# One hybrid MLA + NSA block on one Trainium2 core: weights' low parts summed by accumulating DMAs, short Newton steps moved to GpSimd, strips loaded a step ahead

## The chip, the cores and the metric

The kernel runs on 1 core of one Trainium2 chip. The metric is device microseconds of one execution. The engines are TensorE (PE; its weight loads are PEld), VectorE (DVE), ScalarE (ACT), GpSimd (POOL) and SyncE (SP), which here only issues DMAs.

## What is computed

A decoder block over 512 tokens with D = 1024, all in float32:

```
mod = silu(c) @ ada_w + ada_b                     # six vectors: shift, scale, gate, twice
h   = rms_norm(x) * (1 + sc1) + sh1
z   = h @ w_in                                    # latents c_q (768), c_kv (256), k_pe, the NSA inputs, two merge gates (2 x 1024)
q   = rms_norm(c_q) @ w_q_b                       # 8 heads x 96;  k, v from rms_norm(c_kv) @ w_kv_b
y_mla = causal_attention(norm_rope(q), norm_rope(k), v) @ w_o_mla
y_nsa = (compressed + selected + window attention) @ w_o_nsa
x   = x + gt1 * ((sigmoid(g1) * y_mla + sigmoid(g2) * y_nsa) @ w_out)
h2  = rms_norm(x) * (1 + sc2) + sh2
out = x + gt2 * ((silu(h2 @ w_gate) * (h2 @ w_up)) @ w_down)
```

## The kernel before

Every matrix product is made of three: both factors are split into a high part, rounded to float32r, and a low part, which is the rest, and high x high, high x low and low x high are summed in PSUM. A weight chunk of up to 128 x 1024 is split by `wchunk`: SP loads `raw`, ACT copies it into `whi` (`hi_of`, which rounds), DVE (or POOL) subtracts to give `wlo` (`lo_of`). `raw`, `whi` and `wlo` have four buffers each (pool `wp`), used in turn by all weights and by the strips of `ada_w` (below), so a load waits until the fourth last user of `raw` is done.

The stages, by the span of the profile: input normalisation and the first modulation vectors; the input projection; NSA attention (some 160 to 302 us); the latent stage, 302 to about 350 us, which projects latents to keys and values (`gk`, `use_kv`) and then queries (`gq`, `use_q`, two halves c = 0 and 1 of four heads each); MLA attention over eight heads (about 350 to 450 us); the merge (`gym`), `w_out` (`gwo`, `wo`), the second normalisation (`make_h2`) and the feed-forward part to the end.

Two kinds of work are laid beside the attention. Fillers are PE work with nothing else to do with it: `gates` (16 chunks of the two merge gates, PSUM tile `gp`) and `y_nsa` (tile `yn`). Their results go through an SBUF tile `gs` to DRAM (`spill`) and come back as `gx`, `gm` and `yn`. Their low parts are made by POOL until the end of NSA, by DVE after it (`fill_on`), in two halves of 128 x 512 (`FILL_CUT`). And `mods` computes the other modulation vectors: it loads strips of `ada_w` and sums them, scaled, into `macc` by DVE. The quotas E_MODS, F_MODS, Y_MODS and W_MODS say how many steps of `mods` go into the latent stage, the MLA heads, the merge and `w_out`.

The root mean square of queries and keys is turned into its inverse by `rsqrt`: a guess from the bits and three Newton iterations on a 128 x 16 tile (`rq_i`, `rq_h`, `rq_m`). `rsk` scales the keys `kn`; `rsq` is the scale in the DVE instruction that reads a score tile `ps` out of PSUM and gives `s` and its minimum `mn`.

The program order is not the order of the code: the framework schedules the instructions when it builds, engine by engine, from estimated durations, and each engine then runs its own list strictly in that order. An instruction that waits holds up all behind it on its engine, a DMA issue too.

## Time and profile before

| | |
|---|---|
| median of 3 runs (range) | 886.44 us (884.62 to 892.15) |
| the profiled execution | 885.92 us, of which the span from first to last instruction is 884.1 us |
| PE busy | 842.3 us, 95% of the span |
| DVE / ACT / POOL busy | 681.2 / 451.9 / 98.3 us |
| mean granted TensorE clock | 0.987 of full speed |

All times in the rows below are microseconds from the first instruction of the profiled execution, unless marked ns. An engine's busy time counts what it computes, not the DMAs that it issues.

### The profile page before, as it was taken

What the parts mean: (1) busy time and instruction counts of PE and PEld (TensorE: products, weight loads), DVE (VectorE), ACT (ScalarE), POOL (GpSimd) and SP (SyncE); (2) the same over time, 40 slices, a digit from 0 to 9 for tenths busy, and PEclk for the clock granted to TensorE, in tenths of its full rate; (3) what the DMA queues carried; (4) which work ended last, traced back from release to release, by engine and by line L of the source; (5) the groups of instructions that cost most, each with busy time, mean ns of one, the idle gap of its engine ahead of it and who ended that gap; (6) DMA issues with size and microseconds to landing.
All of it is one profiled execution on the core that took longest, in us unless ns stands there. A gap on an engine that the chain in (4) does not pass through costs nothing.

```text
span 884.1 us, 13839 instructions
## 1 busy us (share of the span) xinstructions
PE 842.3 (95%) x5012; PEld 740.3 (84%) x5012; DVE 681.2 (77%) x1438; ACT 451.9 (51%) x902; POOL 98.3 (11%) x146
## 2 busy tenths in 40 slices
PE   5999899899999999799899989999999999999997
PEld 4889899678777788688788879898999889988996
DVE  5858786678987599679779885996788768865875
ACT  5445664686766564466534255452366326641550
POOL 0004235343442000001010000000000000000000
PEclk9999999799999999899999999999999999999999
DMA  9934455312100455225589762534233413343312
GB/s 314 320 111 125 138 149 137 84 48 61 49 25 24 151 172 172 90 88 164 169 275 314 232 212 73 160 126 121 69 98 97 143 48 97 108 131 96 96 49 95
DMA packets 96217, 115.53 MB, mean 131 GB/s; under 512 B 6564, under 2 KB 68884, under 8 KB 96148
## 3 DMA queue, kind: packets, MB, share of 16 engines
q1 hardware_dynamic: 96052, 114.62, 41.9%
q8 instruction: 39, 0.64, 0.3%
q14 instruction: 30, 0.25, 0.1%
q10 hardware_dynamic: 96, 0.03, 0.0%
...
## 4 chain that ended last, share of the span: by engine, by line
PE 76%; DVE 10%; DMA 8%; ACT 2%; issue 2%; POOL 1%; SPq 1%; DVEq 0%; ACTq 0%
PE d L143 14%; PE fx L143 12%; PE fy L143 9%; PE gp L143 9%; PE ga L143 5%; PE pt L143 3%; PE av L143 3%; DMA raw<-in_ada_w_dram 3%; PE gwo L143 3%; PE gym L143 3%; PE fg L143 3%; PE fu L143 3%; PE wo L143 2%; DVE wlo L143 2%; PE wa L143 2%
## 5 line engine op out<-in xcount | busy, mean ns | idle before, releaser
L143 ACT ACTIVATE whi<-raw 128x1024 fp32r<-128x1024 f32 (+4 forms) x162 | 142.0, 893 | 146.5 <-PE d L143 49.3
L143 DVE TENSOR_TENSOR wlo<-raw,whi 128x1024 fp32r<-128x1024 f32 (+4 forms) x138 | 149.4, 1089 | 65.8 <-ACT whi L143 65.6
L143 PE MATMUL d<-wlo,mh 128*128 128x512 f32 (+1 forms) x180 | 70.7, 393 | 0.0
L143 PE MATMUL d<-whi,mh 128*128 128x512 f32 (+1 forms) x180 | 69.5, 392 | 0.6 <-DVE tm L143 0.5
L143 PE MATMUL d<-whi,ml 128*128 128x512 f32 (+1 forms) x180 | 67.8, 389 | 0.0
L143 ACT ACTIVATE s<-s,mn 128x384 f32<-128x384 f32 (+2 forms) x96 | 52.5, 548 | 26.0 <-DVE mn L143 23.5
L143 DVE TENSOR_TENSOR plo<-pt,phi 128x512 fp32r<-128x512 f32 (+2 forms) x78 | 46.3, 601 | 20.4 <-ACT phi L143 20.1
L143 ACT ACTIVATE phi<-pt 128x512 fp32r<-128x512 f32 (+2 forms) x78 | 40.1, 526 | 33.3 <-PE pt L143 32.7
L143 PE MATMUL gp<-hTh,whi 128*128 128x512 f32 x128 | 55.2, 431 | 0.0
L143 PE MATMUL gp<-hTh,wlo 128*128 128x512 f32 x128 | 51.5, 404 | 0.0
L143 PE MATMUL gp<-hTl,whi 128*128 128x512 f32 x128 | 51.4, 401 | 0.0
L143 ACT ACTIVATE whi<-s 128x1024 fp32r<-128x1024 f32 (+1 forms) x36 | 30.2, 845 | 32.3 <-PE d L143 18.0
L143 POOL TENSOR_SCALAR s<-s,sm 128x512 f32<-128x512 f32 (+3 forms) x40 | 25.0, 637 | 152.7 <-DVE sm L143 67.8
L143 PE MATMUL fx<-h2h,whi 128*128 128x256 f32 x144 | 41.2, 286 | 0.0
L143 PEld LDWEIGHTS d<-whi,mh 128*128 128x128 f32 x180 | 33.7, 188 | 8.9 <-DVE tm L143 1.2
L143 PE MATMUL fx<-h2h,wlo 128*128 128x256 f32 x144 | 40.9, 284 | 0.0
L143 PE MATMUL fx<-h2l,whi 128*128 128x256 f32 x144 | 40.8, 283 | 0.0
L143 PEld LDWEIGHTS d<-whi,ml 128*128 128x128 f32 x180 | 33.8, 188 | 7.9 <-issue 0.2
L143 PEld LDWEIGHTS d<-wlo,mh 128*128 128x128 f32 x180 | 33.8, 188 | 7.7 <-issue 0.2
L143 DVE TENSOR_TENSOR wlo<-s,whi 128x1024 fp32r<-128x1024 f32 (+1 forms) x36 | 33.8, 950 | 7.4 <-ACT whi L143 7.4
L143 DVE SCALAR_TENSOR_TENSOR macc<-raw,csil,macc 128x512 f32<-128x512 f32 x45 | 33.6, 753 | 5.6 <-DMA raw<-in_ada_w_dram 5.3
L143 PE MATMUL pt<-ident,s 128*128 128x128 f32 x232 | 37.8, 282 | 0.0
...
## 6 DMA issues: line engine op xcount, KB each, us to landing
...
araw<-in_ada_w_dram SPq DMA_DIRECT2D x32, 256.0 KB, 6.3
...
spill<-gs SPq DMA_DIRECT2D x24, 256.0 KB, 2.0
...
```

The lines of the kernel that those rows point to most:

```text
L143: out = call(*args, **kw)
```

## The change

- `sum_lo` is new: ACT writes the negated, rounded weights into `wlo`, and a DMA that POOL issues adds `raw` to them in place. It replaces DVE's subtraction in the query projection (`eng_lo=sp` is the mark for it) and, after NSA, in the fillers.
- `rsqrt` can run its Newton steps on another engine: POOL for the keys (`k0`, `k1`) and the queries (`q0`, `q1`). There it takes 12 steps where DVE took 9.
- `use_q` copies all 96 columns of a head out of PSUM by ACT; DVE's rotation then reads SBUF.
- Spills are issued by ACT (gates) and POOL (`yn`), no longer by SP.
- `mods` gives way between a strip's load and its sums, with all quotas doubled to match.
- The low parts of the second half of the first gate and up weights wait until the second piece of `h2` is done.

```diff
@@ -38,11 +38,11 @@
 E0_GATES = 8
 E_GATES = 0
 F_FILL = 64
-E_MODS = 4
-F_MODS = 4
+E_MODS = 8
+F_MODS = 8
 GS_BUFS = 1
-Y_MODS = 4
-W_MODS = 4
+Y_MODS = 8
+W_MODS = 8
 BIG = 1e30
 QL = 768
 KVL = 256
@@ -206,7 +206,8 @@
     pe.transpose(pt[:, :56], vec, ident[:56, :56])
     dve.tensor_copy(out=cols, in_=pt[:, :56])
 
-    def rsqrt(dst, src, pool_, tag):
+    def rsqrt(dst, src, pool_, tag, eng=None):
+        eng = eng or dve
         n = src.shape[-1]
         rows = src.shape[0]
         yi = pool_.tile([P, n], I32, name=f"rq_i_{tag}", tag=f"rq_i{n}", bufs=2)[:rows]
@@ -216,10 +217,14 @@
         dve.tensor_scalar(out=hx, in0=src, scalar1=-0.5, scalar2=None, op0=ALU.mult)
         y = yi.bitcast(F32)
         for it in range(3):
-            dve.tensor_tensor(out=m, in0=y, in1=hx, op=ALU.mult)
-            dve.tensor_tensor(out=m, in0=m, in1=y, op=ALU.mult)
+            eng.tensor_tensor(out=m, in0=y, in1=hx, op=ALU.mult)
+            eng.tensor_tensor(out=m, in0=m, in1=y, op=ALU.mult)
             o = dst if it == 2 else y
-            dve.scalar_tensor_tensor(out=o, in0=m, scalar=1.5, in1=y, op0=ALU.add, op1=ALU.mult)
+            if eng is dve:
+                dve.scalar_tensor_tensor(out=o, in0=m, scalar=1.5, in1=y, op0=ALU.add, op1=ALU.mult)
+            else:
+                eng.tensor_scalar(out=m, in0=m, scalar1=1.5, scalar2=None, op0=ALU.add)
+                eng.tensor_tensor(out=o, in0=m, in1=y, op=ALU.mult)
 
     ss = cst.tile([P, NT + 1], F32, name="ss")
     rstd = cst.tile([P, NT], F32, name="rstd")
@@ -249,6 +254,10 @@
                 act.activation(out=v, in_=v, func=AF.Copy, scale=rstd[:, t : t + 1])
 
     scale_x(0, P)
+
+    def sum_lo(dst, src):
+        act.activation(out=dst, in_=src, func=AF.Copy, scale=-1.0)
+        pool.dma_start(out=dst, in_=src, accum_op=ALU.add)
 
     def wchunk(src, parts, n, eng_lo=None, cut=1):
         raw = wp.tile([P, 1024], F32, name="raw", tag="raw")
@@ -260,7 +269,10 @@
         for i in range(cut):
             c = slice(i * m, (i + 1) * m)
             hi_of(h[:, c], raw[:, c])
-            lo_of(l[:, c], raw[:, c], h[:, c], eng_lo)
+            if eng_lo is sp:
+                sum_lo(l[:, c], raw[:, c])
+            else:
+                lo_of(l[:, c], raw[:, c], h[:, c], eng_lo)
         return (h[:, : parts * n].rearrange("p (a n) -> p a n", a=parts),
                 l[:, : parts * n].rearrange("p (a n) -> p a n", a=parts))
 
@@ -867,9 +879,10 @@
             gs = wp.tile([P, 1024], F32, name="gs", tag="raw")[:, :S]
         if gate is None:
             act.activation(out=gs, in_=ps, func=AF.Tanh, scale=0.5)
+            act.dma_start(out=spilled[at // 4][at % 4], in_=gs)
         else:
             dve.scalar_tensor_tensor(out=gs, in0=gate, scalar=1.0, in1=ps, op0=ALU.add, op1=ALU.mult)
-        sp.dma_start(out=spilled[at // 4][at % 4], in_=gs)
+            pool.dma_start(out=spilled[at // 4][at % 4], in_=gs)
 
     def ahead(jobs, lead=1, eng=lambda: ()):
         ready = [wchunk(*job, *eng()) for job in jobs[:lead]]
@@ -946,6 +959,7 @@
                 for r0 in range(0, KD, 2):
                     raw = strip()
                     sp.dma_start(out=raw.rearrange("p (r n) -> p r n", r=2), in_=rows(ada, r0 * P, 2, m * D + hf * S, S))
+                    yield
                     for r in range(2):
                         src = raw[:, r * S : (r + 1) * S]
                         c = csil[:, r0 + r : r0 + r + 1]
@@ -1072,7 +1086,7 @@
     nsa_last = pe.log[-1]
     spill_src.clear()
     pe.pace = 0
-    fill_on[0] = dve
+    fill_on[0] = sp
     tab_st.close()
 
     mc_st = scope()
@@ -1126,13 +1140,13 @@
                 pv = ps.rearrange("p (h d) -> p h d", h=4)
                 jq = mp.tile([P, 4, MQK], F32, name="jq", tag="jq", bufs=2)
                 act.activation(out=jq, in_=pv, func=AF.Square)
-                act.activation(out=qn[t][:, hs, 0:64], in_=pv[:, :, 0:64], func=AF.Copy)
+                act.activation(out=qn[t][:, hs, :], in_=pv, func=AF.Copy)
                 rot = mp.tile([P, 4, 32], F32, name="rot", tag="rot", bufs=2)
                 heads = lambda v: v.unsqueeze(1).broadcast_to([P, 4, v.shape[-1]])
                 qr = qn[t][:, hs, 64:96]
-                dve.tensor_tensor(out=rot[:, :, 0:16], in0=pv[:, :, 80:96], in1=heads(snq[:, t, 0:16]), op=ALU.mult)
-                dve.tensor_tensor(out=rot[:, :, 16:32], in0=pv[:, :, 64:80], in1=heads(snq[:, t, 16:32]), op=ALU.mult)
-                dve.tensor_tensor(out=qr, in0=pv[:, :, 64:96], in1=heads(c2q[:, t, :]), op=ALU.mult)
+                dve.tensor_tensor(out=rot[:, :, 0:16], in0=qr[:, :, 16:32], in1=heads(snq[:, t, 0:16]), op=ALU.mult)
+                dve.tensor_tensor(out=rot[:, :, 16:32], in0=qr[:, :, 0:16], in1=heads(snq[:, t, 16:32]), op=ALU.mult)
+                dve.tensor_tensor(out=qr, in0=qr, in1=heads(c2q[:, t, :]), op=ALU.mult)
                 dve.tensor_tensor(out=qr, in0=qr, in1=rot, op=ALU.add)
                 dve.tensor_reduce(out=msq[:, c, t, :], in_=jq, axis=AX.X, op=ALU.add)
             return f
@@ -1140,7 +1154,7 @@
         def norm_q(c):
             hs = slice(4 * c, 4 * c + 4)
             dve.scalar_tensor_tensor(out=msq[:, c], in0=msq[:, c], scalar=1.0 / MQK, in1=each_t(vq, 4), op0=ALU.mult, op1=ALU.add)
-            rsqrt(flat(rsq[:, c]), flat(msq[:, c]), mt, f"q{c}")
+            rsqrt(flat(rsq[:, c]), flat(msq[:, c]), mt, f"q{c}", pool)
             yield
 
         def use_kv(c):
@@ -1159,7 +1173,7 @@
                     mk, rk = msk[:, c], rsk[:, c]
                     dve.tensor_tensor(out=mk, in0=mk, in1=each_t(rkv2, 4), op=ALU.mult)
                     dve.tensor_tensor(out=mk, in0=mk, in1=each_t(skp, 4), op=ALU.add)
-                    rsqrt(flat(rk), flat(mk), mp, f"k{c}")
+                    rsqrt(flat(rk), flat(mk), mp, f"k{c}", pool)
                     for u in range(NT):
                         dve.tensor_tensor(out=kn[u][:, hs, 64:96], in0=kpr[:, u : u + 1, :].broadcast_to([P, 4, 32]),
                                           in1=rsk[:, c, u, :].unsqueeze(2).broadcast_to([P, 4, 32]), op=ALU.mult)
@@ -1176,7 +1190,7 @@
         qk_st = scope()
         qkp = qk_st.enter_context(tc.tile_pool(name="qkp", bufs=2, reuse_waits="tile"))
         for c in range(2):
-            with_side(gemm_tok(sel_ct(0), a["mla_w_q_b"][0], 6, 384 * c, 384, use_q(c), tag=f"q{c}"))
+            with_side(gemm_tok(sel_ct(0), a["mla_w_q_b"][0], 6, 384 * c, 384, use_q(c), tag=f"q{c}", eng_lo=sp))
             if c == 0:
                 run(norm_q(0))
 
@@ -1411,8 +1425,10 @@
                     act.activation(out=h2, in_=src, func=AF.Identity, scale=a2, bias=b2)
                     hi_of(hi, h2)
                 lo_of(lo, h2, hi)
-            yield
-
+            h2_done.append(dve.last)
+            yield
+
+    h2_done = []
     act.gate = act.last
     act.activation(out=warm, in_=ones[:, 0:1], func=AF.Silu)
     act.gate = None
@@ -1599,7 +1615,9 @@
             for k0 in range(0, KD, 4):
                 for nm, w in GU:
                     if q == 0:
+                        dve.gate = h2_done[1] if k0 > 0 else None
                         wt[nm, k0] = wchunk(rows(w, k0 * P, 4, 0, 256), 4, 256)
+                        dve.gate = None
                     gu_matmuls(ps, nm, k0, wt[nm, k0], slice(2 * q * P, (2 * q + 2) * P), q == 0)
                     yield ps
 
@@ -1670,7 +1688,7 @@
                         next(slabs)
                         gated_sums()
                     finish_mid(0, sg_first)
-                run(mix((slabs, 6), (part(mods_gen, 4), 4)))
+                run(mix((slabs, 6), (part(mods_gen, 8), 8)))
         if i == 0:
             run(mods_gen)
             need_mod(5)
```

How it moves instructions. Names: `macc` and `raw<-in_ada_w` belong to `mods`, `ql` and `kl` are low parts of a head's queries and keys, `jq` holds squares, `ISA s,mn<-ps` reads a score tile.

DVE where the first MLA scores are read, before:

```order
L143 TENSOR_SCALAR rq_i_q_4266<-msq 128x16
L143 TENSOR_SCALAR rq_h_q_4267<-msq 128x16
L143 TENSOR_TENSOR rq_m_q_3926<-rq_m_q_3926,rq_i_q_3924 128x16
L143 SCALAR_TENSOR_TENSOR kl<-pt,cols_688,kh 96x512
L143 SCALAR_TENSOR_TENSOR macc<-raw,csil,macc 128x512
L143 TENSOR_TENSOR rq_m_q_4268<-rq_i_q_4266,rq_h_q_4267 128x16
L143 SCALAR_TENSOR_TENSOR rsq<-rq_m_q_3926,rq_i_q_3924 128x16
L143 TENSOR_TENSOR wlo<-raw,whi 128x512 x2
L143 SCALAR_TENSOR_TENSOR macc<-raw,csil,macc 128x512
L143 TENSOR_TENSOR rq_m_q_4268<-rq_m_q_4268,rq_i_q_4266 128x16
L143 ISA s_4123,mn<-ps,mask,rsq 128x128
L143 ISA mn 128x1
```

The same place on DVE now:

```order
L143 SCALAR_TENSOR_TENSOR kl<-pt,cols_688,kh 96x512
L143 SCALAR_TENSOR_TENSOR msq<-msq,vq 128x16
L143 TENSOR_TENSOR qn_3486<-qn_3486,c2q 128x4x32
L143 SCALAR_TENSOR_TENSOR macc<-raw,csil,macc 128x512
L143 TENSOR_SCALAR rq_i_q_4290<-msq 128x16
L143 TENSOR_SCALAR rq_h_q_4291<-msq 128x16
L143 TENSOR_TENSOR qn_3486<-qn_3486,rot 128x4x32
L143 SCALAR_TENSOR_TENSOR macc<-raw,csil,macc 128x512
L143 ISA s_4142,mn<-ps,mask,rsq 128x128
L143 ISA mn 128x1
```

The Newton steps and the filler's low parts are gone from DVE ahead of the first score; two strip sums are still ahead of it.

ACT while it empties the first key/value tiles (`gk`) and splits the first query chunks, before:

```order
L143 ACTIVATE jq<-gk_3557 128x4x64
L143 ACTIVATE kn_3488<-gk_3557 128x4x64
L143 ACTIVATE VM_3492<-gk_3557,rkv 128x4x64
L143 ACTIVATE whi<-raw 128x768
L143 ACTIVATE jq<-gk_3558 128x4x64
L143 ACTIVATE kn_3489<-gk_3558 128x4x64
L143 ACTIVATE VM_3493<-gk_3558,rkv 128x4x64
L143 ACTIVATE whi<-raw 128x768
L143 ACTIVATE jq<-gk_3559 128x4x64
```

The same place on ACT now:

```order
L143 ACTIVATE whi<-raw 128x768
L143 ACTIVATE wlo<-raw 128x768
L143 ACTIVATE jq<-gk_3559 128x4x64
L143 ACTIVATE kn_3488<-gk_3559 128x4x64
L143 ACTIVATE VM_3492<-gk_3559,rkv 128x4x64
L143 ACTIVATE jq<-gk_3560 128x4x64
L143 ACTIVATE kn_3489<-gk_3560 128x4x64
L143 ACTIVATE VM_3493<-gk_3560,rkv 128x4x64
L143 ACTIVATE wlo<-raw 128x768
L143 ACTIVATE whi<-raw 128x768
```

Each chunk of the query weights now has two passes of ACT, and they stand between the evictions of the `gk` tiles.

POOL in the same stretch now (none of these rows stood on it before):

```order
L143 TENSOR_TENSOR rq_i_k_3767<-rq_m_k_3769,rq_i_k_3767 128x16
L143 TENSOR_TENSOR rq_m_k_3769<-rq_i_k_3767,rq_h_k_3768 128x16
L143 TENSOR_TENSOR rq_m_k_3769<-rq_m_k_3769,rq_i_k_3767 128x16
L143 TENSOR_SCALAR rq_m_k_3769<-rq_m_k_3769 128x16
L143 TENSOR_TENSOR rsk<-rq_m_k_3769,rq_i_k_3767 128x16
L260 DMA wlo<-raw 128x768 x3
L143 TENSOR_TENSOR rq_m_q_3937<-rq_i_q_3935,rq_h_q_3936 128x16
L143 TENSOR_TENSOR rq_m_q_3937<-rq_m_q_3937,rq_i_q_3935 128x16
L143 TENSOR_SCALAR rq_m_q_3937<-rq_m_q_3937 128x16
L143 TENSOR_TENSOR rq_i_q_3935<-rq_m_q_3937,rq_i_q_3935 128x16
L143 TENSOR_TENSOR rq_m_q_3937<-rq_i_q_3935,rq_h_q_3936 128x16
L143 TENSOR_TENSOR rq_m_q_3937<-rq_m_q_3937,rq_i_q_3935 128x16
```

The accumulating transfers of the query weights and the keys' Newton steps share POOL's queue.

DVE at the start of the feed-forward part, before (`tm` and `x` finish the second residual half, `h2f` and `h2l` belong to `make_h2`):

```order
L143 TENSOR_SCALAR xs<-x_0_5456,r_5491 128x1024
L143 TENSOR_TENSOR wlo<-raw,whi 128x1024 x2
L143 TENSOR_TENSOR tm<-wo_5744,gt_4625 128x512
L143 TENSOR_TENSOR tm<-wo_5745,gt_4625 128x512
L143 TENSOR_TENSOR x_2_5458<-x_2_5458,tm 128x512
L143 TENSOR_TENSOR x_3_5459<-x_3_5459,tm 128x512
L143 TENSOR_TENSOR wlo<-raw,whi 128x1024
L143 TENSOR_SCALAR h2f_5479<-pt,modc 128x256
```

The same place on DVE now:

```order
L143 TENSOR_SCALAR xs<-x_0_5490,r_5525 128x1024
L143 TENSOR_TENSOR wlo<-raw,whi 128x1024
L143 TENSOR_TENSOR tm<-wo_5778,gt_4651 128x512
L143 TENSOR_TENSOR tm<-wo_5779,gt_4651 128x512
L143 TENSOR_TENSOR x_2_5492<-x_2_5492,tm 128x512
L143 TENSOR_TENSOR x_3_5493<-x_3_5493,tm 128x512
L143 TENSOR_SCALAR h2f_5513<-pt,modc 128x256
L143 TENSOR_SCALAR h2f_5514<-pt,modc 128x256
L143 TENSOR_TENSOR h2l_5495<-h2f_5513,h2h_5494 128x256
```

One low part, 128 x 1024, is still ahead of `tm`; the two others now come behind `h2l`.

## Rows read from the trace of the kernel before

**Rows 1.** Windows by stage: length, busy us (instructions) per engine, PEclk, DMA share, GB/s.

```profile
302.00:318.00 16.00, 14.40 (x69) 10.84 (x67) 14.29 (x26) 13.26 (x31) 0.00 (x0) 1.00 0.75 227
318.00:333.30 15.30, 13.01 (x74) 12.69 (x73) 13.67 (x57) 6.46 (x14) 0.00 (x0) 0.99 0.44 119
333.30:350.00 16.70, 16.70 (x88) 16.36 (x89) 15.19 (x55) 7.62 (x19) 0.00 (x0) 0.91 0.53 151
350.00:364.00 14.00, 9.76 (x46) 7.79 (x45) 11.84 (x43) 6.40 (x16) 0.27 (x1) 0.87 0.66 223
364.00:400.00 36.00, 34.17 (x184) 28.35 (x182) 25.66 (x64) 20.99 (x52) 3.81 (x5) 0.96 0.19 59
400.00:450.00 50.00, 45.96 (x254) 37.96 (x253) 42.62 (x99) 30.06 (x69) 5.59 (x6) 1.00 0.59 190
...
521.00:548.00 27.00, 24.41 (x203) 23.84 (x202) 19.49 (x48) 16.59 (x32) 0.00 (x0) 1.00 0.34 105
```

**Rows 2.** Timeline of PE: start, length, instruction, [idle before it <- releaser].

```profile
318.03 0.44 PE L143 MATMUL gq<-whi,cTh 128*128 128x384 f32 x1
...
333.21 0.66 PE L143 MATMUL gq<-whi,cTh 128*128 128x384 f32 x1 [2.29 <-ACT jq L143]
...
359.60 0.44 PE L143 MATMUL ps<-kh,qh 96*128 96x384 f32 x1 [4.15 <-DVE mn L143]
...
439.16 0.50 PE L143 MATMUL ps<-kh,qh 96*128 96x512 f32 x1 [1.18 <-DVE mn L143]
...
525.78 0.66 PE L143 MATMUL pt<-ident,xs 128*128 128x128 f32 x4 [1.86 <-ACT h2f L143]
```

**Rows 3.** Timeline of DVE, the same columns.

```profile
330.24 1.82 DVE L143 TENSOR_TENSOR wlo<-raw,whi 128x768 fp32r<-128x768 f32 x2
...
332.79 0.28 DVE L143 TENSOR_TENSOR qn<-gq,c2q 128x128 f32<-128x128 f32 x1
...
356.40 0.75 DVE L143 SCALAR_TENSOR_TENSOR macc<-raw,csil,macc 128x512 f32<-128x512 f32 x1 [0.60 <-DMA raw<-in_ada_w_dram]
...
357.15 0.17 DVE L143 SCALAR_TENSOR_TENSOR rsq<-rq_m_q,rq_i_q 128x16 f32<-128x16 f32 x1
...
438.02 0.69 DVE L143 SCALAR_TENSOR_TENSOR gs<-gx,yn 128x512 f32<-128x512 f32 x1 [1.50 <-DMA gx<-spill]
...
523.45 1.22 DVE L143 TENSOR_TENSOR wlo<-raw,whi 128x1024 fp32r<-128x1024 f32 x1
...
524.59 0.99 DVE L143 TENSOR_SCALAR h2f<-pt,modc 128x256 f32<-128x256 f32 x2
```

**Rows 4.** Timeline of ACT, the same columns.

```profile
313.64 0.91 ACT L143 ACTIVATE whi<-raw 128x768 fp32r<-128x768 f32 x1
```

**Rows 5.** Instruction groups: form, count | busy us, mean ns | idle before.

```profile
L143 DVE TENSOR_TENSOR wlo<-raw,whi 128x768 fp32r<-128x768 f32 x6 | 5.6, 950 | 0.0
...
L143 DVE TENSOR_TENSOR rq_m_q<-rq_m_q,rq_i_q 128x16 f32<-128x16 f32 x6 | 1.0, 169 | 0.0
...
L143 DVE TENSOR_TENSOR wlo<-raw,whi 128x512 fp32r<-128x512 f32 x16 | 10.5, 684 | 0.3 <-ACT whi L143 0.3
...
L143 ACT ACTIVATE whi<-raw 128x512 fp32r<-128x512 f32 x40 | 22.8, 622 | 5.0 <-PE gp L143 4.3 <-PE ga L143 0.3 <-PE gq L143 0.3
...
L143 ACT ACTIVATE whi<-raw 128x768 fp32r<-128x768 f32 x6 | 5.2, 863 | 7.5 <-PE gq L143 7.3
```

**Rows 6.** Timeline of POOL in the input projection, same operation twice.

```profile
125.55 1.28 POOL L143 TENSOR_TENSOR rp_nk<-UK,nsin_t 128x32 f32<-128x32 f32 x1
126.79 0.25 POOL L143 TENSOR_TENSOR rp_nk<-UK,sin_t 128x32 f32<-128x32 f32 x1
```

**Rows 7.** DMA issues: count, size each, median us from issue to landing.

```profile
spill<-gs SPq DMA_DIRECT2D x24, 256.0 KB, 2.0
...
raw<-in_mla_w_q_b_dram SPq DMA_DIRECT2D x6, 384.0 KB, 3.2
```

**Rows 8.** Timeline of SP's DMA queue, one spill.

```profile
438.74 0.32 SPq L872 DMA_DIRECT2D spill<-gs  x1
```

## The prediction

> **What bounds the kernel now.** I read the table of windows first, since a share over the whole span mixes stages. From 364 on, and in most stages, PE is busy nearly all the time and only the sum of its matmuls counts; the change takes none of them away. So I look only for time in which PE stands still or runs slow, and only in the stages that the change touches [rows 1]. Length less PE's busy time gives 1.60, 2.29, 0, 4.24, 1.83 and 4.04 us idle in the six windows from 302 to 450: 14.0 us. In three of them the granted clock is below full: 0.91 over 16.7 busy us, 0.87 over 9.76, 0.96 over 34.17, which costs about 1.5, 1.3 and 1.4, together 4.2. From 521 to 548 another 2.59 us are idle. That makes 20.8 us, 2.3% of the time: more cannot come of this change.
>
> PE's timeline then says where the idle time lies [rows 2]. Before 333.21 it waited 2.29 us, by the profile for the square of a query tile by ACT. But the PSUM tile that PE wanted was also read by DVE, in `qn<-gq`, which ended at 333.07, and DVE came to that only after two low parts of 1.82 us [rows 3]. So DVE's queue was the cause. Before 359.60 PE waited 4.15 us for the minimum of a score tile. The first score needs `rsq`, which DVE finished at 357.32; just ahead of its last steps stood a `macc` that waited 0.60 us for a strip of `ada_w` and ran 0.75 [rows 3]. The Newton chain itself is short, 9 steps of 0.17 us [rows 5], but was strewn among other work: the order before shows its last steps between `ql`, `kl` and two `macc`. Both lower clocks follow these two stalls. In the MLA heads the stalls are small and many; the largest kind is 1.18 us at 439.16 [rows 2], where DVE had stood 1.50 us before `gs` for the load of a spilled gate [rows 3].
>
> **The change, part by part.**
>
> *What leaves DVE.* Six low parts of 0.95 us and sixteen halves of 0.684 [rows 5], 5.7 + 10.9 = 16.6 us, and four Newton chains of 9 x 0.17 = 1.5, some 6 us. None of it counts by itself where DVE is not what PE waits for.
>
> *What ACT gets.* A second pass per chunk as long as the first: 6 x 0.863 + 16 x 0.622 [rows 5] = 15.1 us. ACT is busy 13.26 of 16.0 us while it empties the key tiles, and 40 to 60% afterwards [rows 1]. Two of the passes fall into the full stretch.
>
> *What POOL and the DMA engines get.* 22 accumulating transfers. The trace has none, nor any DMA issued by POOL. For the issue the nearest rows are SP's 0.32 us [rows 8] and, above, the longest short POOL operation, 1.28 [rows 6]; I take 1.0, nearer the upper end, since POOL would have to write what SP has made for it. For the transfer: a plain one of 256 KB lands after 2.0 us, one of 384 KB after 3.2 [rows 7]; as it must also read its destination, twice the latter, 6.4, is the upper end. I take 4. None of this can be below nothing.
>
> The Trainium skill (DMA: Bandwidth & Descriptors, Anatomy of one DMA — SWDGE (gpsimd) path) gives about 2.0 us plus bytes over 436 GB/s for a DMA issued by GpSimd, an estimate of 2.9 us for 384 KB; no run here shows it, and the sum below would be 1.1 us better by it.
>
> *First query matmuls.* PE starts them at 318.03 [rows 2], and the first PSUM tile takes the first two chunks in a row, so the second chunk's low part is wanted six matmuls of 0.18 later, at 319.1. ACT rounded that chunk at 313.64 [rows 4]. In the new order the negated pass stands in this place, behind one additional pass of 0.86 for the first chunk: it ends near 313.64 + 0.86 + 0.86 = 315.4. With issue and transfer, 320.4: PE waits **+1.3 us** (bounds 0 and 4.0). The other four chunks have 5 us or more.
>
> *The stall before 333.21.* PSUM is now freed by ACT alone. Next in line is the third tile: there are two `jq` buffers, so its square waits for DVE's reduction of the first, which in DVE's queue stands behind the scaling of the keys, which waits for POOL's Newton steps. Twelve steps cost 12 x 0.25 = 3.0 us at least and 12 x 1.28 = 15.4 at most [rows 6]; I take 4.8, because DVE is partly waiting in that time. This is 3.3 us more than on DVE, and DVE is rid of three low parts ahead of it, 2.85. So it comes out about where it was, with the PSUM release gained: half the stall stays, **-1.1** (bounds +2.0 and -2.29).
>
> *The stall before 359.60.* `rsq` no longer waits for DVE's other work. POOL has from about 340 to 352 for it, with a few DMA issues in between. What is late next is one strip's two `macc` ahead of the first score, 1.4 us and a wait like the 0.60 seen. I leave 1.0: **-3.1** (bounds -1.5 and -4.15). Of the 2.8 us of slow clock behind the two stalls I take **-2.0** (-0.8 and -2.8), as shorter stalls need not end it.
>
> *MLA heads.* Half of the filler halves fall here, 5.5 us of DVE, which is busy 42.6 of 50 us from 400 on [rows 1], and the loads of gates no longer stand behind a spill on SP. The strips, loaded a step ahead, help if their buffers come free in time. Of 5.9 us idle and 1.4 of clock I take **-3.0** (0 and -5). The issue of eight spills on POOL stands ahead of scalings of the probabilities, but those have several us to spare.
>
> *Feed-forward start.* Before 525.78 PE waits 1.86 us; DVE did a low part of 1.22 at 523.45 just ahead of the `h2f` it waited for [rows 2, 3]. That now comes behind: **-1.1** (0 and -1.22). The cover is the first half's weights, ready by then.
>
> *Spills on ACT.* 16 x 0.32 = 5.1 us of ACT if an issue costs there what it costs SP [rows 8], most of it in idle time: **+0.3** (0 and +2).
>
> *Sum.* 1.3 - 1.1 - 3.1 - 2.0 - 3.0 - 1.1 + 0.3 = -8.7 us. The profiled execution took 885.92, 0.5 below the median of 886.44, so **877 us**. A difference of under 1% can't be told from none here; this forecast lies just at that bound, 877.6.
>
> **Rivals.**
>
> *Nearly all idle time goes: 872 us.* If transfers land as plain ones do (2.0 us), the wait of 1.3 is nothing, both stalls and their clock go (-2.3 - 4.15 - 2.8), the heads give 4 and the feed-forward 1.1: -14. For it: DVE then has slack everywhere. Against: ACT is nearly full at 310 to 320. Chance 0.20.
>
> *POOL's Newton steps are what is waited for: 884 us.* The same multiplication of 128 x 32 took 1.28 us and then 0.25 [rows 6]. If most steps take the long time, keys' scaling comes some 10 us later than at my value, part of it covered: the first stall grows by 2.0, the second shrinks by 1.5 only, the clock gives 0.8, the heads 2.0; with +1.3, -1.1 and +0.3 this is -1.8. Chance 0.17.
>
> The Trainium skill (SBUF — State Buffer, Who interferes with whom) says that a DVE instruction with two SBUF inputs shuts GpSimd's reads out for its whole length; the two lengths agree with that, and by this rule this rival would hold wherever DVE is busy with `kn` and `macc`.
>
> *Transfers hold the weight buffers: slower, 896 us.* In the new order 14 SP loads wait for an accumulating transfer, since only four `raw` buffers go round. With 1.3 us of issue and 6.4 of transfer each is 2.7 us later than at my values; if the four buffers cover half, 14 x 1.35 = 19 us. A late strip holds `macc`, and with it the scores behind it on DVE, as at 356.40. It decides as soon as issue and transfer together pass about 7 us; below that the buffers cover it. For it: DMAs wait already now [rows 3]. Against: a fifth to three quarters of the DMA engines' time is used [rows 1], and the fillers are a chunk ahead. Chance 0.15.
>
> **How the numbers follow.** Forecast 0.48, of which 0.26 beyond 1% and 0.22 within; the rivals 0.20 (faster), 0.17 (within) and 0.15 (slower). So faster 0.46, same 0.39, slower 0.15. The range, 870 to 889, takes in the first two rivals and the nearer part of the bounds, and leaves out the slower one and a little below.
>
> **What would show it.** Right: no idle PE before the 13th to 24th query matmuls beyond 1.5 us; the first scores read within 2 us of their matmuls; the clock at or near full from 333 to 364; accumulating transfers landing in 3 to 5 us. Wrong: PE or DVE waiting for `wlo` or for `rsk`; a `macc` waiting over 2 us for a strip; the NSA stage longer because ACT issues spills.

## The result, and the profile after

The changed kernel takes 895.29 us (median of 17 runs, 889.92 to 901.5), the kernel before 888.29 (17 runs beside them): a ratio of **1.0077**, 95% interval 1.0058 to 1.0096. It is slower by some 7 us, where 877 was forecast with a range of 870 to 889.

The profiled execution took 889.92 us with a span of 888.1, only 4.0 more than before. The two profiles already differ ahead of the stages that the change is about: the granted clock was lower in one than in the other from 125 to 180 us (last but two column of the windows; before, then after), and the first key matmul comes at 303.2 instead of 306.1.

```profile
125.00:180.00 55.00, 51.84 (x294) 46.43 (x294) 39.59 (x121) 33.21 (x93) 29.42 (x45) 0.91 0.41 112
```

```profile
125.00:180.00 55.00, 51.76 (x321) 46.63 (x319) 41.32 (x131) 35.21 (x100) 30.14 (x46) 1.00 0.41 112
```

From that matmul to the end it is 578.0 us before and 584.9 after, 6.9 more, which agrees with the medians. So I compare stage by stage, from the first and last start of a group of matmuls. The tile view of the changed kernel gives them (group, count: shortest, median and longest in ns, first to last start in us; shapes):

```profile
L143 PE MATMUL gk<-whi,cTh x16: 389/398/500, 303.2 to 316.8; 128*128 128x512 f32 x16
L143 PE MATMUL gq<-whi,cTh x48: 335/337/445, 317.5 to 342.7; 128*128 128x384 f32 x48
L143 PE MATMUL ps<-kh,qh x32: 223/390/793, 353.4 to 443.8; 96*128 96x128 f32 x8, 96*128 96x256 f32 x8, 96*128 96x384 f32 x8, 96*128 96x512 f32 x8
```

and of the kernel before:

```profile
L143 PE MATMUL gk<-whi,cTh x16: 389/399/504, 306.1 to 317.2; 128*128 128x512 f32 x16
L143 PE MATMUL gq<-whi,cTh x48: 335/338/661, 318.0 to 346.8; 128*128 128x384 f32 x48
L143 PE MATMUL ps<-kh,qh x32: 223/390/629, 352.3 to 439.2; 96*128 96x128 f32 x8, 96*128 96x256 f32 x8, 96*128 96x384 f32 x8, 96*128 96x512 f32 x8
```

The same rows of all the kernels make this table (us; key stage: first `gk` to first `gq`; query stage: first to last `gq`; heads: last `gq` to last `ps`; rest: last `ps` to the end of the span; then DVE's waits at `macc` for strips from 300 to 460):

| kernel | key stage | query stage | heads | rest | `macc` waits |
|---|---|---|---|---|---|
| before | 11.9 | 28.8 | 92.4 | 444.9 | 5.3 |
| after | 14.3 | 25.2 | 101.1 | 444.3 | 22.1 |
| no_sums | 13.0 | 24.7 | 92.1 | 445.4 | 6.4 |
| act_pass | 14.7 | 24.7 | 94.0 | 444.4 | 2.9 |
| quarter | 14.0 | 24.8 | 97.0 | 445.9 | 11.5 |
| q_dve | 13.0 | 24.7 | 102.5 | 444.4 | 15.9 |
| fill_dve | 13.7 | 25.6 | 92.4 | 446.5 | 9.9 |
| load_only | 15.5 | 25.5 | 99.6 | 445.3 | 15.9 |
| load_quarter | 13.8 | 24.7 | 94.1 | 446.3 | 7.4 |
| own_raw | 13.6 | 32.3 | 96.6 | 446.5 | 4.8 |
| before_sums | 14.8 | 27.4 | 110.1 | 447.2 | 25.2 |
| epi_old | 12.9 | 26.2 | 86.0 | 446.4 | 4.6 |

After against before: the query stage gains 3.6, as hoped and more; the key stage loses 2.4 and the heads lose 8.7. Windows over the heads, in the columns of [rows 1], show what the 8.7 are made of (before, then after):

```profile
346.80:439.20 92.40, 82.61 (x448) 68.44 (x446) 74.34 (x192) 54.77 (x131) 7.68 (x9) 0.96 0.42 134
```

```profile
342.70:443.80 101.10, 86.45 (x447) 69.60 (x447) 71.14 (x180) 59.86 (x144) 26.57 (x42) 0.93 0.60 159
```

PE is idle for 14.7 us there, before for 9.8, and its matmuls take 86.5 us instead of 82.6 at a lower granted clock: 4.9 us are waits, and 3.8 are longer matmuls. There is one profile of each kernel, so its rows also carry the chance of where its clock was low; the idle time is the firmer part.

The table of windows of the changed kernel, in the columns of [rows 1]:

```profile
302.00:318.00 16.00, 12.77 (x51) 9.32 (x52) 13.38 (x29) 12.68 (x30) 2.45 (x5) 1.00 0.79 206
318.00:333.30 15.30, 15.07 (x87) 14.75 (x86) 9.95 (x36) 7.89 (x16) 7.71 (x24) 1.00 0.83 199
333.30:350.00 16.70, 14.15 (x74) 12.72 (x73) 10.44 (x38) 12.34 (x26) 9.41 (x19) 0.93 0.99 236
350.00:364.00 14.00, 9.48 (x42) 7.07 (x40) 6.51 (x21) 4.35 (x11) 3.09 (x12) 0.87 0.83 225
364.00:400.00 36.00, 30.86 (x157) 25.21 (x158) 22.12 (x58) 22.78 (x58) 9.02 (x11) 0.89 0.46 110
```

Look at the DMA engines' share first, the last column but one: it is 0.83, 0.99 and 0.83 in the three windows from 318 to 364, where it was 0.44, 0.53 and 0.66 [rows 1]. (The share sums the time of packets; it reads 1.01 in a window of raw6 and 1.06 in one of load_only, so I take a value near 1 for full without knowing the ceiling.) DVE has less to do than before, 10.44 and 6.51 us from 333 to 364, and PE still stands. The clock is low for longer: 0.93, 0.87 and 0.89 over 14.15, 9.48 and 30.86 busy us cost about 1.0, 1.2 and 3.4 us, 5.6 in all, before 4.2. PE's timeline of the changed kernel shows where it stands (the waits that count from 300 to 400):

```profile
311.67 0.50 PE L143 MATMUL gk<-whi,cTh 128*128 128x512 f32 x1 [0.36 <-DVE VM L143]
...
315.98 0.50 PE L143 MATMUL gk<-whi,cTh 128*128 128x512 f32 x1 [1.24 <-DVE VM L143]
...
332.96 0.45 PE L143 MATMUL gq<-whi,cTh 128*128 128x384 f32 x1 [0.23 <-ACT qn L143]
...
347.21 0.50 PE L143 MATMUL gp<-hTh,whi 128*128 128x512 f32 x1 [2.19 <-ACT qn L143]
...
360.29 0.44 PE L143 MATMUL ps<-kh,qh 96*128 96x384 f32 x1 [4.14 <-DVE mn L143]
...
383.71 0.50 PE L143 MATMUL av<-phi,VM 128*128 128x512 f32 x1 [1.91 <-ACT phi L143]
...
396.51 0.50 PE L143 MATMUL av<-phi,VM 128*128 128x512 f32 x1 [1.91 <-ACT phi L143]
```

The stall before 333.21 of [rows 2] is down to 0.23. That before 359.60 is there again with 4.14, and behind it lies another cause. DVE's timeline of the changed kernel:

```profile
343.65 1.54 DVE L143 SCALAR_TENSOR_TENSOR macc<-raw,csil,macc 128x512 f32<-128x512 f32 x2 [5.26 <-DMA raw<-in_ada_w_dram]
...
358.20 0.75 DVE L143 SCALAR_TENSOR_TENSOR macc<-raw,csil,macc 128x512 f32<-128x512 f32 x1 [7.03 <-DMA raw<-in_ada_w_dram]
...
359.88 0.35 DVE L143 CUSTOM_DVE_ANT_0 s<-ps,mask,rsq 128x128 f32<-128x128 f32 x1
```

`macc` waits 7.03 us for a strip, and the first score stands behind it in DVE's list. Before, this wait was 0.60 [rows 3]. What makes the strip late can be read too. These are SP's issues of the strip ahead of the first scores, before and after:

```profile
351.52 0.37 SPq L948 DMA_DIRECT2D raw<-in_ada_w_dram  x1
```

```profile
351.90 0.37 SPq L961 DMA_DIRECT2D raw<-in_ada_w_dram  x1
```

The second came after a wait of SP for an accumulating transfer that held `raw`, one of six that POOL issued from 341.69 on. POOL's timeline, SP's wait (total, times, longest), and the shortest, median and longest time from issue to landing of the six:

```profile
341.69 0.90 POOL L260 DMA_DIRECT2D wlo<-raw  x1 [0.39 <-ACT wlo L143]
...
342.57 1.19 POOL L260 DMA_DIRECT2D wlo<-raw  x1
...
343.54 4.41 POOL L260 DMA_DIRECT2D wlo<-raw  x4
```

```profile
SPq L961 <- DMA wlo<-raw: 4.6, 1, 4.6
```

```profile
DMA to landing us min/median/max: 3.4/6.8/10.7
```

Counted from the first key matmul, the strip was issued after 48.7 us, before after 45.4: 3.3 later. From its issue to the start of `macc` it took 6.3 us, before 4.9: 1.4 more. So `macc` starts 4.7 us later, behind a held buffer and with a slower landing, and DVE was there 1.7 us earlier than before. The waits of the changed kernel's DVE and DMA queue from 300 to 460 (total, times, longest):

```profile
DVE macc L143 <- DMA raw<-in_ada_w_dram: 22.1, 9, 7.0
```

```profile
SPq L961 <- DMA wlo<-raw: 34.7, 6, 12.1
SPq L265 <- DMA wlo<-raw: 24.2, 6, 10.8
```

So two things are to be told apart. SP waits 34.7 us for accumulating transfers ahead of strip loads (L961), since the transfers hold `raw`: that is the mechanism of my slower rival. And the DMA engines are full, or nearly, so that transfers and loads both take longer. The DMA issues of the changed kernel (count, size each, median us from issue to landing) and its queues (packets, MB, share of 16 engines):

```profile
q1 hardware_dynamic: 92596, 108.32, 39.4%
q0 software_dynamic: 3808, 8.65, 4.9%
...
wlo<-raw POOLq DMA_DIRECT2D x16, 256.0 KB, 4.3
...
wlo<-raw POOLq DMA_DIRECT2D x6, 384.0 KB, 4.9
...
raw<-in_w_o_nsa_dram SPq DMA_DIRECT2D x4, 512.0 KB, 10.1
```

A load of the `yn` fillers' weights lands after 10.1 us; before it was 4.0, by this row:

```profile
raw<-in_w_o_nsa_dram SPq DMA_DIRECT2D x4, 512.0 KB, 4.0
```

### The profile page after: what moved, and what is told of

Same layout as the page of the kernel before. It is cut to its first block, busy times and chain, and to the rows that moved or that the text cites. A ratio compares the mean times of both kernels' runs of the same rounds, so it can differ in the third digit from the quotient of the medians.

```text
span 888.1 us, 13885 instructions
## 1 busy us (share of the span) xinstructions
PE 841.9 (95%) x5012; PEld 736.8 (83%) x5012; DVE 663.6 (75%) x1380; ACT 463.3 (52%) x924; POOL 135.0 (15%) x224
## 3 DMA queue, kind: packets, MB, share of 16 engines
q1 hardware_dynamic: 92596, 108.32, 39.4%
## 4 chain that ended last, share of the span: by engine, by line
PE 77%; DMA 8%; DVE 7%; ACT 3%; issue 2%; POOL 2%; SPq 1%; ACTq 0%; DVEq 0%
PE d L143 14%; PE fx L143 12%; PE fy L143 9%; PE gp L143 8%; PE ga L143 5%; PE pt L143 4%; PE av L143 3%; DMA raw<-in_ada_w_dram 3%; PE gwo L143 3%; PE gym L143 3%; PE fg L143 2%; PE wo L143 2%; PE fu L143 2%; PE ps L143 2%; DMA wlo<-raw 2%
## 5 line engine op out<-in xcount | busy, mean ns | idle before, releaser
L143 DVE TENSOR_TENSOR wlo<-raw,whi 128x1024 fp32r<-128x1024 f32 (+3 forms) x116 | 133.2, 1152 | 65.8 <-ACT whi L143 64.4
L143 ACT ACTIVATE phi<-pt 128x512 fp32r<-128x512 f32 (+2 forms) x78 | 39.7, 526 | 25.6 <-PE pt L143 24.8
L143 PEld LDWEIGHTS pt<-ident,s 128*128 128x128 f32 x232 | 28.1, 142 | 8.3 <-DVE s L143 1.8
```

Of the source, the lines that this page charges most:

```text
L143: out = call(*args, **kw)
```

## The experiments

Three theories stood at the start. **A:** the transfers make the strips late, and DVE stands at `macc` with the scores behind it; later this was split into **A1**, they hold the `raw` buffers, and **A2**, their bytes fill the DMA engines. **B:** ACT's second pass is the price. **C:** the loss lies in the other parts, POOL's Newton steps above all. Ratios are to the kernel before, with the 95% interval.

### All sums back on DVE (no_sums), and the two parts of a sum apart (act_pass, pool_neg)

no_sums:

```diff
-    fill_on[0] = sp
+    fill_on[0] = dve
...
-            with_side(gemm_tok(..., use_q(c), tag=f"q{c}", eng_lo=sp))
+            with_side(gemm_tok(..., use_q(c), tag=f"q{c}"))
```

> The changed kernel with all 22 low parts back on DVE: no accumulating transfer and no second pass of ACT; Newton steps on POOL, spills on ACT and POOL, the new query epilogue, the strips a step ahead and the gate in the feed-forward stay. Theory A (the transfers hold the four raw buffers, so strips of ada_w come late and DVE stands at macc): SP waits for no accumulating transfer, macc waits for strips fall from 22 us in 300 to 460 to under 8, and the time is below before, ratio 0.993 to 0.998. Theory B (ACT's second pass is the price): the same ratio, but with macc waiting for strips as in the changed kernel. Theory C (the loss lies in the other parts of the change, POOL's Newton steps above all): ratio stays at 1.005 or more.

act_pass, in `sum_lo`:

```diff
-        pool.dma_start(out=dst, in_=src, accum_op=ALU.add)
+        dve.tensor_tensor(out=dst, in0=src, in1=f32v(dst), op=ALU.add)
```

> The changed kernel with ACT's negated copy kept, and raw added to it by DVE in place of the accumulating transfer: the same work on DVE as before the change, ACT's second pass on top, no transfer. Theory A: without transfers the strips come in time; ratio 0.996 to 1.001, at most 2 us above the kernel with all sums on DVE. Theory B: ACT's second pass costs 4 us or more over the kernel with all sums on DVE; ratio 1.002 to 1.007. Theory C: 1.007.

pool_neg, in `sum_lo`:

```diff
-        act.activation(out=dst, in_=src, func=AF.Copy, scale=-1.0)
+        pool.tensor_scalar(out=dst, in0=src, scalar1=-1.0, scalar2=None, op0=ALU.mult)
```

> The changed kernel with the negated copy for the accumulating transfers made by POOL, not by ACT; the transfers stay. Theory A (transfers hold raw buffers): little is won, ratio 1.004 to 1.008, and DVE still stands some 7 us for the strip ahead of the first scores. Theory B (ACT's second pass delays the emptying of key tiles, qn and phi): the three stalls in the key projection of the changed kernel (0.41, 0.36 and 1.24 us), the 2.19 us before the first gate matmuls and about 1 us per head go; ratio 0.998 to 1.001. Theory C: no change, 1.007.

Measured: no_sums **0.9974** (0.9949 to 0.9998), act_pass **1.0007** (0.9978 to 1.0036), pool_neg **1.0204** (1.0173 to 1.0236). Without the sums by transfers the rest of the change is a small gain, and theory C falls. act_pass, whose list on PE has about half as many lines of difference from the changed kernel's as that of no_sums, is 0.7% faster than the changed kernel: that is what the transfers cost, as far as the lists agree. It is 0.3% above no_sums, with overlapping intervals; its rows are 1.7 us longer in the key stage (14.7 against 13.0) and 1.9 in the heads, the price of ACT's second pass together with that of other lists. pool_neg came out above every range and didn't separate anything: POOL takes longer for the negation than ACT, 1.48 us at least where ACT takes 0.62 for its rounding [rows 5], and PE waits 2.1 us for `wlo` behind it:

```profile
L143 POOL TENSOR_SCALAR wlo<-raw x20: 1478/1494/2200, 312.9 to 420.3; 128x512 fp32r<-128x512 f32 x14, 128x768 fp32r<-128x768 f32 x6
```

### More buffers (raw6, own_raw)

raw6, in all four places:

```diff
-    name="raw", tag="raw")
+    name="raw", tag="raw", bufs=6)
```

> The changed kernel with six raw buffers where it has four; nothing else is changed. Theory A: strips are loaded before they are needed, macc waits for strips fall below 8 us in 300 to 460, PE's wait of 4.14 us before 360 shrinks below 1.5; ratio 0.999 to 1.003. Theory B: the strips come earlier, but ACT still delays keys and phi; ratio 1.003 to 1.007. Theory C: 1.007.

own_raw, in `wchunk`:

```diff
-        raw = wp.tile([P, 1024], F32, name="raw", tag="raw")
+        own = {"tag": "rawx", "bufs": 2} if eng_lo is sp else {"tag": "raw"}
+        raw = wp.tile([P, 1024], F32, name="raw", **own)
```

> The changed kernel with two raw buffers of their own for the chunks whose low parts come by transfers, so that strips, spilled tiles and other chunks have the four to themselves. Theory A1 (a transfer holds a buffer that a strip needs): SP no longer waits for transfers ahead of strips, DVE's waits at macc fall below 8 us in 300 to 460, ratio 0.999 to 1.003. Theory A2 (the DMA engines are full from 318 to 364, so that every load lands later, whoever has a buffer): the waits at macc stay above 14 us and the ratio at 1.005 or more.

Measured: raw6 **1.0144** (1.0115 to 1.0172), own_raw **1.0146** (1.0104 to 1.0187). More room made it slower: raw6 lies above every range, and own_raw has the ratio of A2 with the waits of A1. In raw6 SP fetched further ahead, the DMA engines were at 0.98, 0.91 and 1.01 from 318 to 364, and DVE still stood 23.6 us at `macc`. In own_raw the strips came in time (`macc` waits 4.8, as theory A1 wanted), though as many bytes were moved; but the two buffers held back the query weights themselves: PE waited 5.2 us for `wlo`, and the query stage took 32.3 us. Both were scheduled anew from the start and also lost time ahead of the key stage, in stretches of lower clock, so their totals say little. Their rows say that more buffers don't cure it; that held buffers have no part in the late strips they don't say, rather the opposite.

### Which transfers (q_dve, fill_dve)

Each is one of the two edits of no_sums alone.

> The changed kernel with the six low parts of the query weights back on DVE; the sixteen halves of the fillers still come by ACT's second pass and accumulating transfers. If the price lies with the fillers' transfers, which overlap the strips around the first scores, the ratio stays at 1.003 to 1.007 and DVE still stands several us for strips from 333 to 364; if the query's transfers bring it, the ratio falls to 0.997 to 1.001.

> The changed kernel with the fillers' low parts back on DVE; the six transfers of the query weights stay. If the fillers' transfers are the price: ratio 0.998 to 1.001, the key projection still some 1.5 us longer than with all sums on DVE (ACT's second pass), the MLA heads as with all sums on DVE. If the query's transfers are: 1.004 to 1.007.

Measured: q_dve **1.0050** (1.0024 to 1.0077), fill_dve **0.9950** (0.9919 to 0.9981). The price lies with the sixteen halves of the fillers, their transfers and ACT's passes together, which run beside the strips around the first scores: with them the heads take 102.5 us, without them 92.4. The six transfers of the query weights alone can't be told from DVE's sums (no_sums), and this version, below the range expected, is 0.5% faster than the kernel before.

### The load alone, and a quarter of it (load_only, load_quarter, quarter)

load_only makes every sum on DVE, and beside it adds the rounded part to a spare tile. Only the next transfer into the same place depends on that, and ACT's next rounding into the `whi` buffer that is read; in the trace no engine stands for one:

```diff
+    idle_to = cst.tile([P, 2048], F32, name="idle_to")
...
+    def sum_lo(dst, src, hi):
+        lo_of(dst, src, hi)
+        n = src.shape[-1]
+        at = idle_at[0] % (2048 // n) * n
+        idle_at[0] += 1
+        o = idle_to[:, at : at + n]
+        pool.dma_start(out=o, in_=f32v(hi), accum_op=ALU.add)
```

> The kernel with all sums on DVE, and beside them 22 accumulating transfers of the same sizes, whose result nobody uses: they add the rounded part to a spare tile, so that they hold no raw buffer and no matmul waits for them; ACT makes no second pass. Theory A1: as with all sums on DVE, ratio 0.996 to 0.999. Theory A2: the load on the DMA engines alone brings most of the transfers' price of 6 us, ratio 1.001 to 1.005, strips landing later than with all sums on DVE.

load_quarter cuts both ends of that transfer to a quarter:

```diff
-        o = idle_to[:, at : at + n]
-        pool.dma_start(out=o, in_=f32v(hi), accum_op=ALU.add)
+        o = idle_to[:, at : at + n // 4]
+        pool.dma_start(out=o, in_=f32v(hi)[:, : n // 4], accum_op=ALU.add)
```

> The kernel with the 22 idle accumulating transfers, each cut to a quarter of its columns: as many issues, in the same order on every engine, a quarter of the bytes. Theory A2 (bytes on the DMA engines delay the loads): most of the 7 us over the kernel with all sums on DVE goes, ratio 0.997 to 1.001, the loads of the fillers land in 4 to 5 us again. Theory D (POOL's issues and the other order bring the price): ratio stays at 1.003 to 1.007.

quarter does the same with the transfers of the changed kernel itself, and so leaves out three quarters of the additions:

```diff
-        pool.dma_start(out=dst, in_=src, accum_op=ALU.add)
+        n = src.shape[-1] // 4
+        pool.dma_start(out=dst[:, :n], in_=src[:, :n], accum_op=ALU.add)
```

> The changed kernel with each accumulating transfer cut to a quarter of its columns, so that three quarters of the low parts lack the addition of raw; issues, ACT's second pass and all but a few places of the order are the same. If the bytes are the price: ratio 0.996 to 1.001, macc waits for strips below 12 us in 300 to 460, the loads of w_o_nsa land in 4 to 6 us, not 10. If issue, ACT's pass or the order are: 1.005 to 1.008.

Measured: load_only **1.0054** (1.0025 to 1.0082), load_quarter **0.9926** (0.9899 to 0.9952), quarter **1.0009** (0.9983 to 1.0036). load_only lies just above the range of A2, load_quarter below both ranges. These two have the same lists on PE, ACT and SP row for row, and as many issues by POOL; on DVE four `macc` and two others stand one to three places apart. So 1.3% is the bytes, or nearly. no_sums has the lists of PE and SP row for row too: against it load_only is 0.8% slower, the more careful figure, and load_quarter is not slower, so the 22 issues by themselves cost nothing that shows. Nothing in load_only holds a `raw` buffer, ACT makes no second pass and no matmul needs what is moved; yet its heads take 99.6 us, nearly as long as in the changed kernel. load_only's DMA issues and DVE's waits at strips, and then load_quarter's:

```profile
idle_to<-whi POOLq DMA_DIRECT2D x16, 256.0 KB, 6.5
...
raw<-in_w_o_nsa_dram SPq DMA_DIRECT2D x4, 512.0 KB, 6.9
```

```profile
DVE macc L143 <- DMA raw<-in_ada_w_dram: 15.9, 8, 4.1
```

```profile
idle_to<-whi POOLq DMA_DIRECT2D x16, 64.0 KB, 4.3
...
raw<-in_w_o_nsa_dram SPq DMA_DIRECT2D x4, 512.0 KB, 5.2
```

```profile
DVE macc L143 <- DMA raw<-in_ada_w_dram: 7.4, 4, 2.3
```

In the changed kernel, with few places moved, the cut gives back 0.7%, to the place of act_pass. Its `w_o_nsa` loads land after 3.6 us, and the 4.14 us before the first scores are gone. But a smaller transfer also holds its `raw` buffer for less time: the six transfers ahead of the first scores land after these times (shortest, median, longest) where it was 6.8 in the median:

```profile
DMA to landing us min/median/max: 2.4/3.6/4.9
```

So quarter shows what the transfers cost, by bytes and held buffers together; that bytes alone can cost as much, load_only shows. What is left in its heads is hardly idle time, 10.5 us against 9.8 before; the matmuls take longer at a lower clock:

```profile
344.20:441.20 97.00, 86.49 (x446) 70.09 (x445) 70.33 (x178) 60.05 (x144) 25.47 (x41) 0.93 0.48 138
```

Two waits for ACT remain at the same matmuls as in the changed kernel:

```profile
380.51 0.50 PE L143 MATMUL av<-phi,VM 128*128 128x512 f32 x1 [1.91 <-ACT phi L143]
...
393.31 0.50 PE L143 MATMUL av<-phi,VM 128*128 128x512 f32 x1 [1.91 <-ACT phi L143]
```

### The other parts, on no_sums (newton_dve, epi_old, strips_old)

newton_dve:

```diff
-            rsqrt(flat(rsq[:, c]), flat(msq[:, c]), mt, f"q{c}", pool)
+            rsqrt(flat(rsq[:, c]), flat(msq[:, c]), mt, f"q{c}")
...
-                    rsqrt(flat(rk), flat(mk), mp, f"k{c}", pool)
+                    rsqrt(flat(rk), flat(mk), mp, f"k{c}")
```

> The kernel with all sums on DVE, and the four Newton chains back on DVE too. If the chains on POOL bring the gain over before (my term of the second stall, -3.1 us): ratio 0.999 to 1.002, a longer wait ahead of the first scores. If the new query epilogue brings it: 0.996 to 0.998 as with the chains on POOL. If POOL's chains are waited for (the rival of 884 us): lower, 0.993 to 0.996.

epi_old, the `use_q` of before:

```diff
-                act.activation(out=qn[t][:, hs, :], in_=pv, func=AF.Copy)
+                act.activation(out=qn[t][:, hs, 0:64], in_=pv[:, :, 0:64], func=AF.Copy)
...
-                dve.tensor_tensor(out=qr, in0=qr, in1=heads(c2q[:, t, :]), op=ALU.mult)
+                dve.tensor_tensor(out=qr, in0=pv[:, :, 64:96], in1=heads(c2q[:, t, :]), op=ALU.mult)
```

> The kernel with all sums on DVE, and the query epilogue as before the change: DVE reads the rope columns from PSUM. If this read was what held PE before 333 (my term of the first stall): PE stands again for 1.5 to 2.5 us in the query projection with a lower clock behind, ratio 1.000 to 1.003. If not: no such stall, 0.997.

strips_old, in `mods`, with all quotas at 4 again:

```diff
                     sp.dma_start(out=raw.rearrange("p (r n) -> p r n", r=2), in_=rows(ada, r0 * P, 2, m * D + hf * S, S))
-                    yield
```

> The kernel with all sums on DVE, and each strip again loaded in the step that sums it, with the counts of steps of before. If loading a step ahead helps: macc waits longer for strips than the 6 us in 300 to 460, ratio 0.999 to 1.003. If the four buffers and SP's order undo it anyway: the same as with it, 0.996 to 0.998.

Measured: newton_dve **0.9944** (0.9911 to 0.9976), epi_old **0.9859** (0.9837 to 0.9881), strips_old **0.9954** (0.9934 to 0.9974), just below its lower range. Beside no_sums (0.9949 to 0.9998) neither the chains on POOL nor the strips a step ahead can be told from nothing, though the value of newton_dve lies in the range that stood for chains that are waited for. epi_old is the surprise: the stall that the old epilogue brings back is there (1.21 us at 331.62, behind DVE's `qn`), its query stage is 1.5 us longer than in no_sums, and yet it is the fastest kernel of all, 1.4% below the kernel before, because its heads take 86.0 us instead of 92.1. By this window (as above) PE is idle for 3.4 us of them; in no_sums it is 10.2:

```profile
343.80:429.80 86.00, 82.56 (x447) 68.40 (x446) 71.73 (x177) 53.59 (x128) 15.44 (x27) 0.96 0.46 144
```

### Parts in other company (all_epi_old, before_epi, before_sums, epi_newton_old, epi_spill_old)

These use the same edits again: all_epi_old is the whole change with the edit of epi_old; before_epi puts the new `use_q` alone into the kernel before, before_sums `sum_lo` with its two marks alone; epi_newton_old is epi_old with the edit of newton_dve. New is only epi_spill_old, epi_old with the spills on SP again:

```diff
-            act.dma_start(out=spilled[at // 4][at % 4], in_=gs)
...
-            pool.dma_start(out=spilled[at // 4][at % 4], in_=gs)
+        sp.dma_start(out=spilled[at // 4][at % 4], in_=gs)
```

> The whole change with the old query epilogue. If the prices add: 1.0077 less 1.1%, ratio 0.995 to 0.999. If the transfers alone set the MLA heads: ratio stays at 1.003 to 1.008.

> The kernel before with the new query epilogue alone. By my prediction's first stall it gains 1 to 4 us: ratio 0.995 to 0.999, no stall of 2.29 us ahead of 333. If the epilogue costs by itself what it costs with all sums on DVE: the stall goes, the MLA heads get longer, ratio 1.004 to 1.012.

> The kernel before with the accumulating transfers and ACT's second pass alone. If their price is the same here as in the changed kernel (7 us of transfers, 2 to 3 of ACT's pass): ratio 1.006 to 1.013, the loads of the fillers landing in 7 us or more. If they need the other parts: 0.997 to 1.002.

> All sums on DVE, the old query epilogue and the Newton chains on DVE: of the change there stay the strips a step ahead, the spills on ACT and POOL, and the gate in the feed-forward. If the chains on POOL earn my 3 us: ratio 0.989 to 0.993. If they earn nothing: 0.983 to 0.988 as with them.

> All sums on DVE, the old query epilogue, Newton chains on POOL, and the 24 spills issued by SP again. By my term (+0.3 us for the spills on ACT, with loads no longer behind a spill on SP inside the -3.0 of the heads): ratio 0.986 to 0.990. If the spills on ACT and POOL bring the gain: 0.992 to 0.997.

Measured: all_epi_old **1.0077** (1.0047 to 1.0107), before_epi **0.9995** (0.9967 to 1.0023), before_sums **1.0190** (1.0158 to 1.0223), epi_newton_old **0.9986** (0.9957 to 1.0014), epi_spill_old **0.9894** (0.9858 to 0.9930). before_sums lies above all its ranges, epi_newton_old too, and before_epi between its two. In before_epi the query stage is 3.5 us shorter by the new epilogue, but its heads take 97.3 us instead of 92.4, so nothing is left of it. The sums by transfers, ACT's pass with them, cost in every company: 1.9% on the kernel before, 1.0% on no_sums (to the whole change), 2.2% on epi_old (to all_epi_old). The epilogue and the chains don't add up: with sums on DVE the four pairs give 0.9974 (new, POOL), 0.9944 (new, DVE), 0.9859 (old, POOL) and 0.9986 (old, DVE). Every such edit makes the scheduler write new lists (against no_sums, epi_old and newton_dve each have several hundred lines of difference on PE alone, the numbers of tiles left out), and where a waiting `macc` falls in them can move more than the edit does. In no_sums the strip that SP issued at 352.04 holds DVE for 2.11 us at 356.74, between the score tiles; in epi_old the one issued at 356.75 is not waited for at 360.79, after a wait of 1.30 ahead of the first score. What in the four lists makes 86.0 us of heads in one and 92 to 94 in the others is not settled by these runs.

The spills on ACT and POOL (epi_old against epi_spill_old, overlapping intervals) show no difference.

## Why the prediction was wrong, point by point

**The step that failed** is "What POOL and the DMA engines get". Its two prices were about right in the median: POOL's issue took 0.94 us (the 20 from 300 on; I took 1.0), the transfers landed after 4.3 and 4.9 us (I took 4). What failed is that I charged them only to whoever waits for `wlo`, and nothing to the rest: the sum has no term for 6.55 MB (16 x 256 KB and 6 x 384 KB) on DMA engines that the loads also need. Of the queue's 4.9% of sixteen engines, 0.6 belongs to the eight spills (no_sums has these alone), so 4.3% of 16 x 888.1, 611 engine-us (microseconds of one engine's time, summed), moved 6.55 MB: 93 per MB. The loads took 39.4% for 108.32 MB, 52 per MB. A byte of an accumulating transfer costs the engines 1.8 times that of a load, and sixteen of the 22 fall where the strips are wanted. In their densest burst the transfers themselves took up to 10.7 us, and so held `raw` longer as well. load_only and load_quarter show that the bytes alone cost 0.8 to 1.3%; quarter, that with a quarter of them the changed kernel gets 0.7% back. For the strip ahead of the first scores the issue came 3.3 us later, behind a held buffer, and the landing took 1.4 longer; how the whole loss divides between the two stays open.

By the Trainium skill (DMA: Bandwidth & Descriptors, Anatomy of one DMA — SWDGE (gpsimd) path) a transfer of 384 KB was an estimate of 2.9 us; the accumulating one took 4.9, so the measurement is above it, as it was above my 4.

**First query matmuls, +1.3:** nothing. PE starts them at 317.48 and doesn't wait. But the key stage ahead of them is 2.4 us longer, and PE waits 0.36 and 1.24 us before `gk`. One of ACT's second passes, which I saw fall "into the full stretch" and priced at nothing, stands ahead of the first. The second wait, the longer one, is a late strip again: DVE's `VM` came behind two `macc` that had waited 1.14 us, when ACT's own part of the tile was done at 314.39:

```profile
313.83 0.56 ACT L143 ACTIVATE VM<-gk,rkv 128x256 fp32r<-128x256 f32 x1
```

```profile
313.66 1.54 DVE L143 SCALAR_TENSOR_TENSOR macc<-raw,csil,macc 128x512 f32<-128x512 f32 x2 [1.14 <-DMA raw<-in_ada_w_dram]
...
315.44 0.47 DVE L143 SCALAR_TENSOR_TENSOR VM<-gk,rkv,VM 128x256 fp32r<-128x256 f32 x1
```

act_pass, without transfers, has a key stage 1.7 us longer than no_sums, but there too the longest wait, 1.45 us, ends at DVE, behind a strip 0.81 us late and DVE's own sums. How much of it is ACT's pass is not shown.

**The stall before 333.21, -1.1:** it went whole, with the slow clock behind it, 3.6 us for the stage. The PSUM release by ACT does it: before_epi has a query stage of 25.3 us by the epilogue alone. That DVE's reduction would come late behind POOL's steps did not happen: the steps of the keys took 0.21 to 0.48 us, a chain of twelve 4.9 (I took 4.8), `kn` waited 1.86 for them, and PE for none of it. So the rival of 884 us falls at its place and by its price; only one step of the queries took 1.30.

**The stall before 359.60, -3.1:** nothing gained. I named what would be late next, one strip's two `macc`, and gave it 1.0; it was late by 7.03 at `macc` and 4.14 at PE. In its neighbourhood came a new wait of 2.19 before 347.21, where ACT does four passes for the fillers, two of them second passes, ahead of the square and copy that free a query tile. Without the second passes, in no_sums, it is 1.12:

```profile
342.87 0.50 PE L143 MATMUL gp<-hTh,whi 128*128 128x512 f32 x1 [1.12 <-ACT qn L143]
```

**Clock, -2.0:** +1.4 by the windows (5.6 against 4.2), since the stalls behind it moved from the query stage into the heads.

**MLA heads, -3.0:** they and the second stall together lost 8.7 us. The strips "help if their buffers come free in time": they didn't, and DVE's relief of 5.5 us was worth nothing while it waited. The two waits of 1.91 us before `av` come with two of ACT's second passes each, 1.1 us, ahead of the exponentials, which I had put into idle time; in no_sums the waits at `av` are 0.95 us at most.

**Feed-forward start, -1.1:** right in kind. PE's wait of 1.86 [rows 2] became one of 0.88 at 529.38 behind `h2l` and one of 0.20 at 543.10: 0.8 gained.

**Spills on ACT, +0.3:** they cost 0.33 us each, and no difference shows.

**The slower rival** had the sign, the place (a late strip ahead of the scores) and a price close to the result, and I gave it 0.15; that price went by a guess that the four buffers cover half, so its closeness is luck. Its mechanism, held buffers, is there: SP waited 58.9 us for transfers, and the strip ahead of the first scores was issued only after one of them. Its point was issue and transfer together above 7 us; in the median they were 5.2 to 5.8, but in that burst the transfer alone took 6.8 in the median. What it lacked is the reason: it set 6.4 as the upper end of a single transfer, while the runs show a burst that lengthens its own transfers and the loads beside them. Nor are held buffers needed: with none held, load_only loses nearly as much, and quarter keeps SP's waits for transfers at 47.5 us and still gives the 0.7% back. What I held against it, that only "a fifth to three quarters" of the DMA engines' time is used, was the fault: I read the share as room, and not what a busier engine does to the landing time of the next load.
